# Issuing seven weight loads from GpSimd's queue instead of SyncE's, in a convolution and attention step

## The chip, the cores and the metric

The program runs on one core of a Trainium2 chip. The metric is the device time of one execution in microseconds (us), the median of several runs. Five engines run their own instruction streams in the order in which the program was scheduled: TensorE (PE, with PEld for its weight loads), VectorE (DVE), ScalarE (ACT), GpSimd (POOL) and SyncE (SP, which here does nothing but issue transfers). An engine that waits for an instruction's inputs lets nothing behind it in its stream pass. Transfers between the chip's memory and the on-chip buffer are issued from one of these streams and carried out by 16 DMA engines.

## The reference, cut to what matters

The program is one inference step of a two-layer decoder. The first layer is a gated convolution; the part that matters here is its end:

```python
h = _rmsnorm(x, g_norm)
val, glu_gate, z = jnp.split(h @ w_in, 3, axis=-1)
v = val * jax.nn.sigmoid(glu_gate)
c = depthwise_conv(v, 31 taps) + conv_b
c = jax.nn.silu(_layernorm(c, ln_g, ln_b))
y = (c * jax.nn.silu(z)) @ w_out        # (2080 x 2048) @ (2048 x 1024)
x1 = x + y
```

After it come a shared key/value product, dilated window attention in three groups and an output product, which the change does not touch. All values are float32.

## The kernel before, in words

**Precision.** A float32 product is made of three products in a format that TensorE reads at full rate. Each operand is split into a high part (a cast) and a low part (the rest). The output weights `w_out` arrive raw, tile by tile; ACT casts the high part (`ho`, line 262), and DVE or POOL subtracts to get the low part (`lo`, line 265). DVE takes both halves of the first tile and the second halves of the next three, POOL the others.

**Stages around the change.** Phase A computes the products of `w_in` and the convolution. Its last part, `tail`, multiplies the three last column tiles of z with the five chunks of x (`zchunk`, lines 73 to 77); ACT applies silu and issues the store. Between the chunks `phase_b` puts the first two row tiles through the layer norm. Phase B has 17 row tiles of 128 rows (the last but one has 32), in "positions" 0 to 16. For each position:

- `norm` loads c (`bc`, line 297) and silu(z) (`bsz`, line 303), reduces over channels (DVE, line 306), finishes the mean by a product with a matrix of constants (PE, line 308, into `bst`), subtracts (DVE, line 309), squares in two halves (ACT, line 312, into the one buffer `bsq`), reduces each half (DVE, line 314, `bv`), finishes the variance on PE (line 315), takes the root and reciprocal (ACT line 317, DVE line 318), multiplies (DVE, line 319), applies silu with gain and bias (ACT, line 321, 16 pieces) and multiplies with silu(z) (DVE, line 322).
- `split` makes the high part `bmh` (ACT, line 336) and the low part `bml` (DVE, line 337).
- `out` makes two output products of 48 matmuls each (lines 359 to 361, into `bpo`), one per half j of the 1024 output columns.

**The weights.** `w_out` is 2048 x 1024, cut into j = 0, 1 and four tiles each (h = 0 to 3), a tile being 1 MB. `Weights.ahead` (line 234) loads seven of these eight raw tiles in two transfers of 512 KB each; the eighth goes through a stage of its own in `Weights.half` (line 257). In the names below, the raw tiles of j = 0 are `rawo_9236`, `rawo_9239`, `rawo_9242` and `rawo_9245` with the high parts `ho_9248`, `ho_9254`, `ho_9260`, `ho_9266`; those of j = 1 are `rawo_9312`, `rawo_9315`, `rawo_9318`. `bc_8798`, `bc_8926`, `bc_9272`, `bc_9464` and `bc_9616` are the c tiles of positions 0, 1, 2, 3 and 4. The raw tiles lie in memory that x held in phase A. So the first can be loaded when chunk 0 of z is done, the other three of j = 0 when chunk 1 is done, and those of j = 1 when all of z is done.

**What sets the order.** A scheduler at build time plays the program through with a cost model and writes each engine's stream as it goes; nothing is reordered on the chip. Priorities steer it: loads and casts of weights are made with `high_priority(offset=1000)`. The variable `pace` holds the last transfer of a chain, and `issue_after(pace)` keeps a transfer behind that one. In the kernel before, the raw loads and the loads of c (line 297) are in this chain, all in SP's stream.

Of the kernel before, what the change touches and what calls it, by code (L numbers as in the profile page):

```python
# [224 lines left out]
class Weights:  # L225
# [8 lines left out]
    def ahead(self, src, nm, tag, pool=None):  # L234

        raw = (pool or self.pool).tile([128, 4, 512], F32, tag=tag, name=f"raw{nm}")
        with self.tc.high_priority(offset=1000):
            for q in range(2):
                with self.tc.issue_after(self.d["pace"].ins):
                    self.d["pace"] = self.nc.sync.dma_start(raw[:, 2 * q:2 * q + 2], src[q])  # L240
        return raw

    def half(self, src, nm, gain=None, pool=None, raws=None):
# [33 lines left out]
def phase_b(tc, d, kc, tail, outer, then):  # L277
# [6 lines left out]
    with ExitStack() as ctx:  # L284
# [90 lines left out]
        def ahead(c):  # L375
            if c < 2:
                cc[c] = norm(c)
                if c == 0:
                    ms[0] = split(0, cc[0])

        tail(ahead)
        pw = outer.enter_context(tc.tile_pool(name="w", bufs=1, side="right", reuse_waits="tile"))
        wts = Weights(tc, d, pw, outer.enter_context(tc.tile_pool(name="w_s", bufs=2, side="right", reuse_waits="tile")))
# [733 lines left out]
```

## Time and profile before

| | us |
|---|---|
| median of 3 runs | 3110.9 |
| lowest and highest | 3108.03, 3112.82 |
| the profiled execution | 3108.9 |
| its span in the trace | 3107.1 |
| PE busy in it | 2990.2 (96%) |
| DVE, ACT, POOL busy | 2187.3, 1517.9, 1281.0 |

The span is the time from the first to the last recorded instruction; the execution is 1.8 us longer. The page cuts the span into 40 slices of 77.7 us and shows PE's busy share of each in tenths. Five slices are below nine tenths: the first, while the input is prepared; the one from 1087.5 to 1165.2 us (seven tenths), in which phase A hands over to phase B; the one from 1320.6 us (seven tenths) in phase B; and two in the attention stage, the very last among them. The raw tiles are loaded in the hand-over, and the rows below are mostly of it and of the 100 us behind it.

### The profile page before, as it was taken

The page shows a single profiled execution, that of the slowest core. Times are in us where ns is not written, and L with a number is a line of the kernel's source. Part 1 is how long each engine was busy: PE and PEld are TensorE (multiplying, and loading weights), DVE is VectorE, ACT ScalarE, POOL GpSimd, SP SyncE. Part 2 cuts the span into 40 slices and gives each one's busy share as a digit, 9 for nine tenths or more (in the row PEclk, how much of TensorE's full clock was granted, in tenths as well). Part 3 has the DMA queues.
Part 4 walks back from the last instruction along what each step waited for, and adds up shares of the span by engine and source line. Part 5 has one row for each costly group of instructions (what it writes and reads, how often), then busy time and mean ns, then how long its engine had stood idle before and what let it go on. Part 6 is the DMA issues. An engine that isn't in the chain of part 4 may idle for free.

```text
span 3107.1 us, 43111 instructions
## 1 busy us (share of the span) xinstructions
PE 2990.2 (96%) x15994; PEld 2537.2 (82%) x15994; DVE 2187.3 (70%) x3698; ACT 1517.9 (49%) x2913; POOL 1281.0 (41%) x809
## 2 busy tenths in 40 slices
PE   6999999999999979999979999999999998999998
PEld 6999999999999977878756777767777776667786
DVE  6599999999999957667556565666666756445355
ACT  6544555554544355566544444554444633444432
POOL 1799889888877603000013222223332032002242
PEclk9999999999999999999999999999999999999999
DMA  7333334434331266444386666788766566653674
GB/s 196 99 107 100 121 106 144 139 112 134 112 128 64 79 194 192 125 133 119 99 211 183 168 164 171 174 232 212 180 162 153 171 189 187 186 182 116 247 258 161
DMA packets 563404, 482.41 MB, mean 155 GB/s; under 512 B 338321, under 2 KB 474129, under 8 KB 555641
## 3 DMA queue, kind: packets, MB, share of 16 engines
q1 hardware_dynamic: 560601, 475.64, 52.2%
q10 hardware_dynamic: 2592, 4.01, 0.4%
q8 instruction: 126, 2.06, 0.3%
q14 instruction: 85, 0.70, 0.1%
HBM read 345.42 MB, written 221.84 MB: 183 GB/s over the span
## 4 chain that ended last, share of the span: by engine, by line
PE 57%; DVE 14%; DMA 11%; POOL 9%; issue 4%; ACT 4%; SPq 1%; POOLq 0%; DVEq 0%; ACTq 0%
DVE acc L196 7%; POOL ca L181 7%; PE s L808 3%; PE pjk L536 3%; DMA qb<-t_qs 3%; PE pjk L539 2%; PE pjk L538 2%; PE pjv L536 2%; PE pt L827 2%; PE pjv L539 2%; PE ut L836 2%; PE pjv L538 2%; PE pjq L538 2%; PE pjq L536 2%; PE pjq L539 2%
## 5 line engine op out<-in xcount | busy, mean ns | idle before, releaser
L181 POOL TENSOR_TENSOR ca<-ca,tp 128x1024 f32<-128x1024 f32 x288 | 706.7, 2456 | 174.3 <-ACT tp L180 123.7
L196 DVE SCALAR_TENSOR_TENSOR acc<-vb,cws,acc 128x1024 f32<-128x1024 f32 x608 | 754.6, 1281 | 6.5
L180 ACT ACTIVATE tp<-vb,cws 128x1024 f32<-128x1024 f32 x288 | 329.7, 1151 | 286.3 <-POOL ca L181 277.5
L750 POOL COPY ro<-xt 128x512 f32<-128x512 f32 x128 | 151.8, 1193 | 381.8 <-DMA t_xt<-ro 168.6
L629 POOL TENSOR_TENSOR qb<-qb,kc 128x512 f32<-128x512 f32 x96 | 124.5, 1301 | 331.1 <-DMA qb<-t_qs 255.0
L68 PE MATMUL pg<-xh,wh 128*128 128x416 f32 x640 | 227.3, 355 | 2.0 <-ACT xh L151 1.9
L68 PE MATMUL pv<-xh,wh 128*128 128x416 f32 x640 | 225.6, 352 | 1.3 <-DVE vb L109 0.8
L69 PE MATMUL pg<-xl,wh 128*128 128x416 f32 x640 | 225.9, 353 | 0.1
L70 PE MATMUL pg<-xh,wl 128*128 128x416 f32 x640 | 225.9, 353 | 0.0
L68 PE MATMUL pz<-xh,wh 128*128 128x416 f32 x640 | 225.1, 352 | 0.0
L70 PE MATMUL pz<-xh,wl 128*128 128x416 f32 x640 | 224.7, 351 | 0.0
L70 PE MATMUL pv<-xh,wl 128*128 128x416 f32 x640 | 224.6, 351 | 0.0
L69 PE MATMUL pv<-xl,wh 128*128 128x416 f32 x640 | 224.3, 351 | 0.0
L69 PE MATMUL pz<-xl,wh 128*128 128x416 f32 x640 | 224.1, 350 | 0.0
L688 POOL MEMSET spq<- 128x24 f32 x8 | 0.9, 118 | 534.3 <-DMA t_x<-bx 371.9
L819 ACT ACTIVATE sm<-sm,ngm 128x256 f32<-128x256 f32 (+1 forms) x384 | 172.7, 452 | 92.5 <-DVE ngm L816 88.0
L359 PE MATMUL bpo<-ho,bmh 128*128 128x512 f32 x512 | 205.2, 403 | 11.4 <-ACT ho L262 7.8
L360 PE MATMUL bpo<-lo,bmh 128*128 128x512 f32 x512 | 204.2, 399 | 4.2 <-DVE lo L265 3.0
L361 PE MATMUL bpo<-ho,bml 128*128 128x512 f32 x512 | 202.5, 397 | 3.4 <-DVE bml L337 3.4
L830 ACT COPY qp_p<-pt 128x512 f32<-128x512 f32 x150 | 86.3, 584 | 179.9 <-PE pt L827 179.3
L536 PE MATMUL pjk<-hk,xt 128*128 128x512 f32 x384 | 161.5, 421 | 10.1 <-ACT xt L500 9.8
L536 PE MATMUL pjq<-hq,xt 128*128 128x512 f32 x384 | 155.4, 405 | 4.3 <-ACT hnk L547 4.3
(319 smaller groups left out, 7569.7 us busy)
## 6 DMA issues: line engine op xcount, KB each, us to landing
t_xt<-ro SPq DMA_DIRECT2D x128, 256.0 KB
xt<-t_xt SPq DMA_DIRECT2D x32, 1024.0 KB
wr<-in_win SPq DMA_DIRECT2D x48, 512.0 KB
qb<-t_qs SPq DMA_DIRECT2D x96, 256.0 KB
kc<-in_cache SPq DMA_DIRECT2D x72, 256.0 KB
vc<-in_cache SPq DMA_DIRECT2D x72, 256.0 KB
t_c<-ca SPq DMA_DIRECT2D x16, 1040.0 KB
bc<-t_c SPq DMA_DIRECT2D x16, 1024.0 KB
```

Of the source, the lines that this page charges most:

```text
L68: nc.tensor.matmul(ps, lhsT=hi[:, k], rhs=xh[:, k], start=(k == 0), stop=False)
L69: nc.tensor.matmul(ps, lhsT=hi[:, k], rhs=xl[:, k], start=False, stop=False)
L70: nc.tensor.matmul(ps, lhsT=lo[:, k], rhs=xh[:, k], start=False, stop=(k == 7))
L180: nc.scalar.activation(tp, src, AF.Copy, scale=cws[:, ct, j:j + 1])
L181: nc.gpsimd.tensor_tensor(dst, dst, tp, op=ALU.add)
L196: nc.vector.scalar_tensor_tensor(out if j == KT - 1 else acc[h], vt[:, h * 1024 + j:h * 1024 + j + 1024], cws[:, ct, j:j + 1], out if j == ...
L359: nc.tensor.matmul(po[:n], lhsT=mh[:, a], rhs=hi, start=(a == 0), stop=False)
L360: nc.tensor.matmul(po[:n], lhsT=mh[:, a], rhs=lo, start=False, stop=False)
L361: nc.tensor.matmul(po[:n], lhsT=ml[:, a], rhs=hi, start=False, stop=(a == 15))
L536: first = nc.tensor.matmul(ps[:n], lhsT=xh[:, j], rhs=hi[:, j], start=(k == 0), stop=False)
L538: nc.tensor.matmul(ps[:n], lhsT=xh[:, j], rhs=lo[:, j], start=False, stop=False)
L539: nc.tensor.matmul(ps[:n], lhsT=xl[:, j], rhs=hi[:, j], start=False, stop=(k == last))
```

## The change

The two transfers of each raw tile in `ahead` are issued from GpSimd's stream, and they leave the `pace` chain. They neither wait for the last transfer in the chain, nor does the next one wait for them.

```diff
@@ -236,8 +236,7 @@
         raw = (pool or self.pool).tile([128, 4, 512], F32, tag=tag, name=f"raw{nm}")
         with self.tc.high_priority(offset=1000):
             for q in range(2):
-                with self.tc.issue_after(self.d["pace"].ins):
-                    self.d["pace"] = self.nc.sync.dma_start(raw[:, 2 * q:2 * q + 2], src[q])
+                self.nc.gpsimd.dma_start(raw[:, 2 * q:2 * q + 2], src[q])
         return raw
```

The changed file is one line shorter, so its line numbers behind 239 are lower by one: line 308 of before is line 307 of after.

The scheduler now writes other streams on all engines. In GpSimd's stream the 14 transfers stand right behind the last low part of phase A's weights and ahead of every `lo` of the output weights. In SP's stream the load of `bc_9272` (position 2) follows directly on that of `bc_9464` (position 3); before, eight raw loads and a load of silu(z) stood between them.

PE, from the end of the z products, before:

```order
L359 MATMUL bpo_0_9360<-ho_9248,bmh_8838 128x512
L360 MATMUL bpo_0_9360<-lo_9249,bmh_8838 128x512
L361 MATMUL bpo_0_9360<-ho_9248,bml_8839 128x512
L359 MATMUL bpo_0_9360<-ho_9248,bmh_8838 128x512
L360 MATMUL bpo_0_9360<-lo_9249,bmh_8838 128x512
L361 MATMUL bpo_0_9360<-ho_9248,bml_8839 128x512
L359 MATMUL bpo_0_9360<-ho_9248,bmh_8838 128x512
L360 MATMUL bpo_0_9360<-lo_9249,bmh_8838 128x512
```

The same place on PE after the change (`bst_9278` and `bst_9471` belong to the norms of positions 2 and 3):

```order
L358 MATMUL bpo_0_9360<-ho_9248,bmh_8838 128x512
L359 MATMUL bpo_0_9360<-lo_9249,bmh_8838 128x512
L360 MATMUL bpo_0_9360<-ho_9248,bml_8839 128x512
L307 MATMUL bst_9278<-bs_9276,ones 128x128
L307 MATMUL bst_9471<-bs_9469,ones 128x128
L358 MATMUL bpo_0_9360<-ho_9248,bmh_8838 128x512
L314 MATMUL bst_9278<-bv_0_9283,ones 128x128
L359 MATMUL bpo_0_9360<-lo_9249,bmh_8838 128x512
```

The first of these rows is the fourth matmul of the product; three like it stand ahead of it. The last three of the four `L314` rows (the second of `bst_9278`, both of `bst_9471`) stand behind the 18th matmul (two) and the 19th (one), and `bst_9622<-bs_9620` (position 4) behind the 48th, ahead of the second product. Before, all 48 matmuls came first, and then the two rows of `L308` for positions 2 and 3.

DVE, from the low part of the first output tile, before:

```order
L265 TENSOR_TENSOR lo_9249<-rawo_9236,ho_9248 128x1024 x2
L337 TENSOR_TENSOR bml_9350<-bc_8926,bmh_9349 128x2048
L265 TENSOR_TENSOR lo_9255<-rawo_9239,ho_9254 128x1024
L265 TENSOR_TENSOR lo_9261<-rawo_9242,ho_9260 128x1024
L265 TENSOR_TENSOR lo_9267<-rawo_9245,ho_9266 128x1024
L306 TENSOR_REDUCE bs_9276<-bc_9272 128x128
L309 TENSOR_TENSOR bc_9272<-bc_9272,bst_9278 128x2048
```

The same place on DVE after the change:

```order
L264 TENSOR_TENSOR lo_9249<-rawo_9236,ho_9248 128x1024
L336 TENSOR_TENSOR bml_9350<-bc_8926,bmh_9349 128x2048
L305 TENSOR_REDUCE bs_9276<-bc_9272 128x128
L264 TENSOR_TENSOR lo_9261<-rawo_9242,ho_9260 128x1024
L308 TENSOR_TENSOR bc_9272<-bc_9272,bst_9278 128x2048
L308 TENSOR_TENSOR bc_9464<-bc_9464,bst_9471 128x2048
L313 TENSOR_REDUCE bv_0_9283<-bsq_0_9281 128x128
L264 TENSOR_TENSOR lo_9249<-rawo_9236,ho_9248 128x1024
L313 TENSOR_REDUCE bv_1_9288<-bsq_1_9286 128x128
L313 TENSOR_REDUCE bv_0_9476<-bsq_0_9474 128x128
L313 TENSOR_REDUCE bv_1_9481<-bsq_1_9479 128x128
L264 TENSOR_TENSOR lo_9255<-rawo_9239,ho_9254 128x1024
```

The second half of `lo_9249`, which the 8th matmul needs, now stands behind the first three steps of two norms. Next come the two reciprocals, the multiplication of position 2, the second half of `lo_9267`, the multiplication of position 3 and the reduction `bs_9620` of position 4.

ACT, from the first cast of an output tile, before:

```order
L262 CAST ho_9248<-rawo_9236 128x1024 x2
L336 CAST bmh_9349<-bc_8926 128x2048
L262 CAST ho_9254<-rawo_9239 128x1024 x2
L262 CAST ho_9260<-rawo_9242 128x1024 x2
L262 CAST ho_9266<-rawo_9245 128x1024 x2
```

The same place on ACT after the change:

```order
L261 CAST ho_9248<-rawo_9236 128x1024
L335 CAST bmh_9349<-bc_8926 128x2048
L261 CAST ho_9254<-rawo_9239 128x1024
L261 CAST ho_9266<-rawo_9245 128x1024
L261 CAST ho_9260<-rawo_9242 128x1024 x2
L311 ACTIVATE bsq_0_9281<-bc_9272 128x1024
L261 CAST ho_9248<-rawo_9236 128x1024
L311 ACTIVATE bsq_1_9286<-bc_9272 128x1024
L311 ACTIVATE bsq_0_9474<-bc_9464 128x1024
L311 ACTIVATE bsq_1_9479<-bc_9464 128x1024
L261 CAST ho_9254<-rawo_9239 128x1024
```

The second half of `ho_9248` moved behind the first square of position 2, and that of `ho_9254` behind all four squares of positions 2 and 3.

## Rows read from the trace of the kernel before

**Rows 1.** Windows: us; busy of PE, PEld, DVE, ACT, POOL; PE clock; DMA; GB/s.
```profile
1146.00:1176.00 30.00, 15.35 (x51) 11.01 (x52) 24.02 (x9) 18.44 (x28) 12.43 (x4) 0.76 1.10 353
1176.00:1203.00 27.00, 27.00 (x119) 22.22 (x118) 22.16 (x14) 17.79 (x29) 16.96 (x8) 0.95 0.52 173
1203.00:1240.00 37.00, 32.96 (x133) 25.61 (x132) 25.40 (x15) 20.68 (x41) 0.00 (x0) 0.91 0.60 171
1240.00:1560.00 320.00, 312.80 (x1397) 252.93 (x1395) 206.65 (x154) 188.09 (x351) 0.00 (x0) 1.00 0.42 119
```
**Rows 2.** PE's timeline: start, us, instruction, [idle before <-releaser].
```profile
1153.72 0.79 PE L359 MATMUL bpo<-ho,bmh 128*128 128x512 f32 x1 [7.85 <-ACT ho L262]
1157.47 0.79 PE L360 MATMUL bpo<-lo,bmh 128*128 128x512 f32 x1 [2.96 <-DVE lo L265]
...
1159.34 0.63 PE L361 MATMUL bpo<-ho,bml 128*128 128x512 f32 x1
...
1175.29 1.13 PE L308 MATMUL bst<-bs,ones 128*128 128x128 f32 x4 [2.77 <-DVE bs L306]
1176.08 1.20 PE L359 MATMUL bpo<-ho,bmh 128*128 128x512 f32 x2
...
1568.78 0.79 PE L536 MATMUL pjk<-hk,xt 128*128 128x512 f32 x1 [9.16 <-ACT xt L500]
```
**Rows 3.** The timeline of SP's stream of transfers, 1101 to 1164 us.
```profile
1101.12 36.62 SPq L303 DMA_DIRECT2D bsz<-t_sz  x2
...
1143.95 0.36 SPq L297 DMA_DIRECT2D bc<-t_c  x1
1144.43 13.63 SPq L240 DMA_DIRECT2D rawo<-in_wout  x8
...
1161.93 1.88 SPq L297 DMA_DIRECT2D bc<-t_c  x1
```
**Rows 4.** ACT's timeline, four rows from 1099 to 1186 us.
```profile
1099.04 0.52 ACT L76 ACTIVATE st<-pz 128x416 f32<-128x416 f32 x1 [4.02 <-PE pz L70]
...
1152.62 1.99 ACT L262 CAST ho<-rawo 128x1024 fp32r<-128x1024 f32 x2 [0.50 <-ACT st L76]
...
1172.78 1.05 ACT L262 CAST ho<-rawo 128x1024 fp32r<-128x1024 f32 x1 [8.82 <-DMA rawo<-in_wout]
...
1184.47 1.03 ACT L312 ACTIVATE bsq<-bc 128x1024 f32<-128x1024 f32 x1 [1.29 <-DVE bv L314]
```
**Rows 5.** DVE's timeline, eight rows from 1108 to 1192 us.
```profile
1108.75 3.75 DVE L306 TENSOR_REDUCE bs<-bc 128x128 f32<-128x2048 f32 x1 [3.88 <-DMA bc<-t_c]
...
1156.20 2.35 DVE L265 TENSOR_TENSOR lo<-rawo,ho 128x1024 fp32r<-128x1024 f32 x2
1158.47 2.28 DVE L337 TENSOR_TENSOR bml<-bc,bmh 128x2048 fp32r<-128x2048 f32 x1
1160.67 10.08 DVE L265 TENSOR_TENSOR lo<-rawo,ho 128x1024 fp32r<-128x1024 f32 x3
1171.43 3.71 DVE L306 TENSOR_REDUCE bs<-bc 128x128 f32<-128x2048 f32 x1 [0.68 <-DMA bc<-t_c]
1176.04 4.49 DVE L309 TENSOR_TENSOR bc<-bc,bst 128x2048 f32<-128x2048 f32 x2 [0.89 <-PE bst L308]
1180.44 1.22 DVE L314 TENSOR_REDUCE bv<-bsq 128x128 f32<-128x1024 f32 x1
...
1190.39 0.95 DVE L318 RECIPROCAL br<-br 128x128 f32<-128x128 f32 x1 [1.30 <-ACT br L317]
```
**Rows 6.** DMA queues in the window 1172 to 1180 us: packets, MB, share.
```profile
q1 hardware_dynamic: 902, 3.28, 102.6%
```
**Rows 7.** DMA queues in the window 1102.3 to 1104.4 us, SP's (q1), ACT's (q10).
```profile
q1 hardware_dynamic: 1001, 0.50, 84.9%
q10 hardware_dynamic: 142, 0.21, 29.0%
```
**Rows 8.** POOL's timeline, the first low parts of the output weights.
```profile
1159.29 10.39 POOL L265 TENSOR_TENSOR lo<-rawo,ho 128x1024 fp32r<-128x1024 f32 x3 [84.12 <-ACT ho L262]
```

## The prediction

> **What bounds the kernel now.** I read the windows by stage first, then PE's waits in the poorest of them, then what the engines named there were doing, and last the streams of transfers. The windows [rows 1] show where there is anything to gain or lose. In the 30 us after the z products PE is busy for 15.35 us at a granted clock of 0.76; in the next 27 us it is never idle; in the 37 us behind them it lacks 4.0 us (37.00 - 32.96), at a clock of 0.91; in the 320 us after 1240 it lacks 7.2 us. So the hand-over costs about 15 us of idle PE, and what follows is bound by PE.
>
> PE's timeline [rows 2] says what the idle time was. The first wait, 7.85 us up to 1153.72, ends with ACT's cast `ho`. It does not end with a load: ACT's row for that cast [rows 4] starts at 1152.62 behind ACT's own `st`, in the order of its stream. The second, 2.96 us, ends with DVE's `lo`, itself behind a reduction and a multiplication. Only then comes the third, 2.77 us before the `bst` product at 1175.29.
>
> Transfers are late in two places only. DVE's reduction of position 2 (`bc_9272`) starts at 1171.43, when its load lands [rows 5], and ACT is idle for 8.82 us until the raw tiles of j = 1 are there at 1172.78 [rows 4]. SP's stream [rows 3] tells why: it stood at a load of silu(z) for 36.62 us until 1137.7, issued the c tile of position 3 at 1143.95, then eight raw transfers in 13.63 us, and reached `bc_9272` only at 1161.93.
>
> **The change, part by part.** *Issue.* 14 issues leave SP. The ones that could run early do: chunk 1 of z is done at about 1099.04 [rows 4], so seven transfers of 0.524 MB (3.67 MB) start then, some 45 us earlier than at 1144.43. This gains nothing at the first product's start, since ACT's order sets that. On POOL the issues fall into an idle stretch of 84.12 us [rows 8]. No row shows what one costs there: between 0 and the 1.70 us of SP's (13.63 / 8), 14 of them take 0 to 24 us of POOL, most of it ahead of 1159. POOL's `lo` of `ho_9254` stands behind all 14, the last of which wait for the end of z (1145.9 by PE's row at 1153.72 less 7.85): six issues from there last until 1146 to 1156. I take no cost.
>
> *Loads beside each other.* The c tile of position 1 lands at 1108.75, and DVE had waited 3.88 us for it [rows 5]; PE's `bst` of it stands inside the z products. Now 3.67 MB go beside it. At the 410 GB/s of raw loads (3.28 MB in 8 us, [rows 6]) that is 8.9 us of the DMA engines: the upper end, if the c tile waits for all of it. The lower end is 0. The nearest row is of two queues beside each other [rows 7]: the second queue took 0.21 of 0.71 MB, 30%. Of the 9.7 us from 1099.04 to 1108.75 that is 2.9 us: **+3 us** at the end of z.
>
> The Trainium skill bears on this (*DMA: Bandwidth & Descriptors*, section *SWDGE vs HWDGE vs iDMA*): inside each DMA engine the hardware and GpSimd's software queues are served round-robin. The row differs from one packet each in turn: 142 packets passed beside 1001. By the skill's rule with larger packets on GpSimd's side the c tile would wait nearly the whole 8.9 us.
>
> *The order.* This is the large term. SP now issues `bc_9272` right behind `bc_9464`, so the scheduler finds the c tiles of positions 2 and 3 early and writes their norms into the first output product. PE's stream has two `bst` behind the 6th matmul, `bst` again behind the 7th, two behind the 18th, one behind the 19th. These are engines in order, so each such row is a wait of PE for DVE and ACT. In before's clock, from rows 5 unless noted:
>
> 1. PE's sixth matmul ends at 1159.97 [rows 2]. DVE's `bml` ends at 1158.47 + 2.28 = 1160.75. `bc_9272` has landed: two c tiles of 1.05 MB at the 341 GB/s of rows 7 (0.71 MB in 2.1 us) take 6.2 us from 1143.95, and six raw transfers beside them (3.15 MB at 410) another 7.7, to 1157.9.
> 2. DVE's reduction: 3.71, to 1164.5. PE's two `bst`: to 1165.0, after 4.5 us of waiting.
> 3. DVE's `lo_9261` at 3.36 (10.08 / 3, POOL working beside it): 1167.8. Subtraction 2.25 (4.49 / 2): 1170.1. ACT's square 1.03 and cast 1.05 [rows 4]: 1172.2. Only now has the 7th matmul its `ho_9248`: PE waited 7.2 us.
> 4. DVE: the other subtraction to 1172.3, a variance reduction 1.22 to 1173.5, the second half of `lo_9249` (2.35 / 2) to 1174.7, three more variance reductions. The squares share one buffer, so a pair costs 1.03 + 1.22 = 2.25: about 1175.8, 1178.1, 1180.4. PE has its last `bst` at 1180.6.
> 5. ACT casts the second half of `ho_9254` behind the last square; DVE makes `lo_9255` by 1181.7. That is the 20th of 48 matmuls; 29 are left.
> 6. DVE: two reciprocals of 0.95, to 1183.6; a multiplication of some 2.3 (as `bml`, of the same shape) and up to 1 more for POOL beside it, to 1186.5; `lo_9267`, to 1187.7. PE has its next 24 at 0.23 (27.00 / 119, [rows 1]) by 1187.2, and the last five by 1188.8.
> 7. DVE: the multiplication of position 3 to 1190.0, the reduction of position 4 to 1193.7; PE's `bst` for it stands ahead of the second product, which starts at 1194.3.
>
> Before, it started at 1176.08 [rows 2]. **Lag: 18.2 us**, with the loads 21.2. The skeptical end: if the casts hidden by these waits are ready early and the clock no worse, half of steps 3 to 6 is still forced by data, about 9. The other end: with 42 matmuls at half clock, 0.23 us more for each, 9.7 us more, 28.
>
> *What is given back.* The norms of positions 2 and 3 are done some 10 us earlier, relative to the products, than before. So the idle 4.0 us of 1203 to 1240 go [rows 1], as they wait for such norms. The clock of 0.91 there is 18% of 37 us at half speed (6.7 us), which costs 3.3 us; that goes with the idleness. Of the 7.2 us after 1240 I take 2, with bounds 0 and 7.2. Together -9.3 (bounds -4 and -14.5). The eighth raw tile and the j = 1 casts are cast later on ACT, 0 to 4 us; I take 0, since the second product covers them. At the start of the attention stage PE waits 9.16 us for ACT, up to 1568.78 [rows 2]. If what it waits for were independent of the products, up to 9.16 us of lag would vanish there; it is the transposed x1, which the last products make, so I take 0.
>
> Sum: 3 + 18.2 - 9.3 = **+11.9** on the profiled execution's 3108.9: 3120.8. That execution is 2.0 us under the median of the runs (3110.9), so the forecast is **3123 us**.
>
> The skill also has a rule under which nothing of this follows: DMAs from any engine run on the same 16 DMA engines, and issuing from several saves only the sequencer's time (*DMA: Bandwidth & Descriptors*, section *Issuing engines are not separate DMA queues*). The trace differs in one respect: the raw transfers sat behind a wait of 36.62 us in SP's stream, which is order and not issue time [rows 3].
>
> **The rivals.**
>
> *No change to speak of (3108 to 3117).* The norms have to be done anyway, and DVE and ACT have slack later: DVE is busy 206.65 of the 320 us after 1240 [rows 1]. If all the 14.5 us come back and half or none of the lag is covered, the sum is 3 + 9 to 18 - 14.5, -2 to +7; what is above that can still vanish in the 9.16 us at 1568.78. For it: the same work is only moved. Against it: PE lacks only 7.2 us after 1240, so a lag that is left at 1240 has little to be taken out of. If the order mattered little and only issue time were saved, the effect would be the same, as SP's issues are not on PE's path.
>
> *Faster (3104 or below).* The place is positions 2 to 5: norms early enough that no `bst`, `bmh` or `bml` is waited for until the attention stage, 4.0 + 7.2 + 3.3 = 14.5 us gained, with the 2.77 of 1175.29 gone as well, 17.3. It decides when the stalls in the first product are below that less 6.2, about 11; with stalls of 8 the time is 3110.9 + 8 - 17.3 = 3102. For it: both rows that were late on a transfer (1171.43, 1172.78) get theirs 10 us earlier. Against it: steps 2 to 5 are data dependences in PE's stream, 12 us by step 3 alone.
>
> *Much slower (3132).* The raw loads crowd out the c tile of position 1 (8.9 instead of 3) and, with PE idle in pieces, the clock stays at half for the first product (+9.7 at most, 3 taken): 3123 + 5.9 + 3 = 3132. For it: the clock was 0.76 in 1146 to 1176 with PE half idle. Against it: rows 7, where the second queue took 30%.
>
> **How the numbers follow.** Forecast 0.50; much slower 0.20; no change 0.18; faster 0.12. A measurement can tell about 0.2%, 6.2 us, from no change, so "same" is 3104.7 to 3117.1. Faster then 0.11, same 0.19 (with the edge of the faster case), slower 0.70. The range takes the forecast's own spread (3111 to 3135: 3123 less half of the 18.2 us and 3 for the loads, and 9.7 and 2.3 more at half clock) and reaches down into "no change" and up past the crowding: 3107 to 3138. The slow cases' own range is 3115 to 3138.
>
> **What would show it.** Right: PE's rows after the sixth matmul wait 4 to 8 us each for DVE's `bs` and ACT's `ho`; the first product takes about 35 us instead of 22; the second starts 15 to 25 us later; windows behind it have less idle time and a full clock. The raw loads run at 1099 to 1109, and DVE's reduction of position 1 starts at 1110 to 1114. Wrong: `bst` without a wait in the first product; a second product that starts by 1185; or the lag coming back in the attention stage.

## The result, and the profile after

The changed kernel takes 3141.56 us (median of 4 runs, 3138.08 to 3147.2) against 3110.46 in the same session: a ratio of 1.0095 with an interval of 1.0084 to 1.0107, 31.1 us slower. The forecast was 3123 with a range of 3107 to 3138. The direction was right, the size was not. The profiled execution is the slowest of the four, 3147.2 us with a span of 3145.4.

Comparing two traces needs one correction. Starts in phase A, which the change does not touch, differ between executions: ACT's `st` at 1072.6 us in the trace of before stands 6.1 us later in that of after, and between 1.6 us earlier and 7.2 us later in the kernels below. On PE and ACT the order of instructions up to there is the same in all these kernels. A shift in this document is a start in one trace less that in the trace of before, less this offset.

Three windows of after that answer to [rows 1], and two that follow the same work (columns as there):

```profile
1146.00:1176.00 30.00, 19.91 (x94) 17.90 (x93) 17.55 (x9) 22.81 (x41) 2.11 (x4) 0.83 0.74 237
1176.00:1203.00 27.00, 11.30 (x37) 8.35 (x38) 24.52 (x13) 11.25 (x13) 7.99 (x5) 0.62 0.61 165
1203.00:1240.00 37.00, 32.72 (x133) 26.43 (x131) 21.07 (x12) 23.74 (x47) 23.56 (x8) 0.91 0.32 86
...
1235.00:1272.00 37.00, 37.00 (x166) 30.48 (x165) 21.63 (x14) 17.73 (x31) 0.00 (x0) 1.00 0.47 139
1269.50:1589.50 320.00, 312.60 (x1390) 252.27 (x1388) 204.45 (x153) 183.52 (x338) 0.00 (x0) 0.99 0.42 119
```

The 27 us in which PE was never idle before are now its poorest: 11.30 busy at a clock of 0.62. The window at 1235 answers to [rows 1]'s window at 1203: its 4 idle us are gone, as forecast, and PE does 166 matmuls in it instead of 133. The 320 us behind it (1269.5, before 1240) lack 7.4 us, before 7.2: nothing was gained there.

PE's timeline after, the waits of the first output product and ahead of the second (answers to [rows 2]):

```profile
1168.30 0.79 PE L358 MATMUL bpo<-ho,bmh 128*128 128x512 f32 x1 [5.68 <-ACT ho L261]
1172.33 0.80 PE L359 MATMUL bpo<-lo,bmh 128*128 128x512 f32 x1 [3.24 <-DVE lo L264]
1179.13 1.19 PE L307 MATMUL bst<-bs,ones 128*128 128x128 f32 x4 [4.30 <-DVE bs L305]
1190.74 0.80 PE L358 MATMUL bpo<-ho,bmh 128*128 128x512 f32 x1 [10.42 <-ACT ho L261]
...
1211.34 0.77 PE L307 MATMUL bst<-bs,ones 128*128 128x128 f32 x2 [4.28 <-DVE bs L305]
```

The two large waits are the ones that the order made: `bst` of positions 2 and 3 at 1179.13, and the seventh matmul at 1190.74, whose cast stands on ACT behind a square. ACT's row for that square says whom it waits for:

```profile
1188.70 1.03 ACT L311 ACTIVATE bsq<-bc 128x1024 f32<-128x1024 f32 x1 [11.78 <-DVE bc L308]
1189.66 1.03 ACT L261 CAST ho<-rawo 128x1024 fp32r<-128x1024 f32 x1
```

DVE's timeline after (answers to [rows 5]):

```profile
1106.32 3.67 DVE L305 TENSOR_REDUCE bs<-bc 128x128 f32<-128x2048 f32 x1 [14.91 <-DMA bc<-t_c]
1123.51 3.58 DVE L305 TENSOR_REDUCE bs<-bc 128x128 f32<-128x2048 f32 x1 [13.52 <-DMA bc<-t_c]
...
1175.37 3.62 DVE L305 TENSOR_REDUCE bs<-bc 128x128 f32<-128x2048 f32 x1
1178.90 7.57 DVE L264 TENSOR_TENSOR lo<-rawo,ho 128x1024 fp32r<-128x1024 f32 x1
```

The second row is position 1: it starts at 1123.51 (before 1108.75), and DVE waited 13.52 us for the c tile instead of 3.88. POOL's timeline after, the issues and the first low parts (answers to [rows 8]):

```profile
1091.67 0.72 POOL L239 DMA_DIRECT2D rawo<-in_wout  x1 [10.36 <-PE pz L70]
1105.45 3.66 POOL L239 DMA_DIRECT2D rawo<-in_wout  x7 [13.06 <-PE pz L70]
1162.83 2.25 POOL L239 DMA_DIRECT2D rawo<-in_wout  x4 [53.72 <-PE pz L70]
1177.34 1.08 POOL L239 DMA_DIRECT2D rawo<-in_wout  x2 [12.26 <-DMA rawo<-in_wout]
1178.44 6.94 POOL L264 TENSOR_TENSOR lo<-rawo,ho 128x1024 fp32r<-128x1024 f32 x3
```

One load starts when chunk 0 is done, seven more at 1105.45, as soon as chunk 1 is done. An issue costs POOL 0.52 us (3.66 / 7). The first low part stands behind all 14, of which the last two waited for a transfer until 1177.34. It starts 0.46 us ahead of DVE's `lo` at 1178.90, and that one lasts until 1.09 us after POOL's three are done (1186.47 and 1185.38). SP's stream (answers to [rows 3]) and the DMA queues from 1105 to 1124 us, with two rows of issues (the columns there: KB of one, median us to landing):

```profile
1105.94 46.40 SPq L302 DMA_DIRECT2D bsz<-t_sz  x2
1158.61 2.39 SPq L296 DMA_DIRECT2D bc<-t_c  x2
1161.10 4.37 SPq L256 DMA_DIRECT2D rawo<-in_wout  x2
```
```profile
q1 hardware_dynamic: 5112, 2.60, 52.2%
q0 software_dynamic: 1008, 3.67, 49.0%
...
rawo<-in_wout POOLq DMA_DIRECT2D x7, 512.0 KB, 10.0
...
t_sz<-st ACTq DMA_DIRECT2D x2, 208.0 KB
```

GpSimd's queue (q0) moves 3.67 MB in 1008 packets of 3.6 KB; SP's packets, with the c tile, are of 0.5 KB. The raw loads are in after 10.0 us, while the c tile takes until 1123.5.

In the attention stage, PE's waits of after from 1594 to 2060 us (engine, line, waited for, us in total, times, longest):

```profile
PE pjq L535 <- ACT hnk L546: 8.4, 1, 8.4
```

Where the time is lost, by shifts: end of z +8.5, taken at ACT's last `st` (PE's own last z matmul is 10.6 late, but PE's wait behind it is 2.2 us shorter, 5.68 instead of 7.85); the first output product +21.1 more (the second starts at 1211.76, not 1176.08 as in [rows 2]: 35.7, less 6.1 and 8.5); 7.6 back by the start of the ninth output product on PE and 1.3 of that lost again by the last, which leaves 23.3; attention, from the first to the last `xt` of its first group (1568 to 1996 us), +4.6; the rest, +4.2, lies behind that. These are 32.1 us between two executions, behind phase A; the medians are 31.1 apart.

### The profile page after: what moved, and what is told of

Its sections match the earlier page's. It is cut to its first block, busy times and chain, and to the rows that moved or that the text cites. A ratio compares the mean times of both kernels' runs of the same rounds, so it can differ in the third digit from the quotient of the medians.

```text
span 3145.4 us, 43122 instructions
## 1 busy us (share of the span) xinstructions
PE 3000.9 (95%) x15994; PEld 2543.1 (81%) x15994; DVE 2178.5 (69%) x3698; ACT 1519.4 (48%) x2913; POOL 1288.2 (41%) x823
## 4 chain that ended last, share of the span: by engine, by line
PE 72%; DMA 10%; DVE 9%; ACT 3%; POOL 3%; issue 2%; SPq 0%; POOLq 0%; ACTq 0%; DVEq 0%
PE pz L70 3%; PE pz L68 3%; PE pz L69 3%; PE pg L68 3%; PE s L807 3%; PE pg L70 3%; PE pg L69 3%; PE pv L68 3%; PE pv L70 3%; PE pv L69 3%; PE pjk L535 3%; DMA qb<-t_qs 3%; PE pjk L538 2%; PE pjk L537 2%; PE pjv L535 2%; PE pjq L535 2%
```

## The experiments

The account under test ("theory A") has three places of loss: the raw loads beside the c tile of position 1, the norms inside the first output product, and the order at the start of the attention stage. The expectations give rivals letters of their own and say what each is. The table has all runs: median and ratio against before in the same session, and shifts (start of DVE's reduction of position 1; end of z, by ACT's last `st`; end of the output products, by DVE's last addition to one; the change from there to the last `xt` of attention's first group). Each shift is of the one profiled execution of its kernel.

| run | median | ratio [interval] | reduction 1 | z | outputs | attention |
|---|---|---|---|---|---|---|
| after | 3141.6 | 1.0095 [1.0084, 1.0107] | 8.7 | 8.5 | 23.3 | +4.6 |
| e1_order | 3125.2 | 1.0044 [1.0022, 1.0066] | 9.1 | 8.8 | 8.8 | +0.1 |
| e2_late | 3123.4 | 1.0047 [1.0031, 1.0063] | -1.1 | -1.2 | 1.3 | +6.1 |
| e3_both | 3122.5 | 1.0038 [1.002, 1.0055] | -1.2 | -1.4 | 8.4 | -0.6 |
| e4_dummy | 3120.8 | 1.0036 [1.0025, 1.0048] | 8.1 | 7.9 | 7.9 | +1.0 |
| e5_attn | 3142.0 | 1.009 [1.0069, 1.011] | 10.0 | 9.7 | 18.2 | +7.0 |
| e6_dose | 3114.5 | 1.0005 [0.9993, 1.0017] | 3.0 | 2.7 | 2.9 | +1.7 |
| e7_j1 | 3125.0 | 1.004 [1.0026, 1.0054] | -1.4 | -1.6 | 6.4 | +7.3 |
| e8_late_attn | 3120.8 | 1.0026 [1.0016, 1.0036] | -1.9 | -1.9 | 3.6 | +4.3 |
| e9_paced | 3127.6 | 1.0047 [1.0029, 1.0066] | 10.1 | 9.8 | 9.9 | +3.6 |
| e10_paced_late | 3136.7 | 1.0075 [1.0057, 1.0094] | 0.8 | 0.8 | 18.9 | +5.7 |
| e11_sp | 3126.0 | 1.0045 [1.0028, 1.0062] | 1.6 | 1.5 | 13.2 | +5.3 |
| e12_dummy_act | 3115.7 | 1.0008 [0.9999, 1.0018] | 6.4 | 6.1 | 4.4 | +0.3 |
| e13_late_attn2 | 3125.1 | 1.0045 [1.0029, 1.0061] | -1.6 | -1.8 | 0.9 | +2.3 |

Before was 3109.7 for e1 to e4, 3112.2 for e5 to e8, 3112.0 for e9 to e12 and 3110.6 for e13. Single runs of one kernel lie up to 17.5 us apart (e7), so a median of a few says little under 5 us; the shifts decide.

**1. The loads alone.** The kernel before, with seven extra raw loads from GpSimd into free memory; then with three.

```diff
+            if pos == 0:
+                extra = [pm.tile([128, 4, 512], F32, tag=tag, name=f"ex{tag}") for tag in ("mh0", "ml0")]
+                for t in extra:
+                    nc.gpsimd.tensor_copy(t[:1, :, :1], c[:1, :4, :1])
+                for k in range(7):      # e6_dose: range(3)
+                    nc.gpsimd.dma_start(extra[k // 2 % 2][:, k % 2 * 2:k % 2 * 2 + 2], wout[k // 4, k % 4][0])
```

> The kernel before the change, with seven more loads of 512 KB from GpSimd's queue into memory that is free then, issued when the c tile of position 0 has landed; nothing reads them. The order of TensorE's stream is that of before. It measures the cost of the loads beside the c tile of position 1 alone. Theory A: the c tile of position 1 lands 6 to 13 us later, TensorE waits for its sum, the time is 3115 to 3124 us. Rival B (such loads cost nothing, only the order does): 3108 to 3113 us.

> The kernel before the change with three extra loads of 512 KB from GpSimd's queue beside the c tile of position 1, instead of the seven of the run named e4_dummy. Theory A (what counts is the bytes that go ahead of the c tile, 1.3 us for each load at 410 GB/s): the c tile lands about 3.5 to 4.5 us late instead of 8.1, the time is 3112 to 3116 us. Rival F (a fixed cost as soon as GpSimd's queue is in use): 7 to 9 us late as with seven, 3117 to 3122 us.

DVE's row for position 1 with seven loads:

```profile
1120.85 3.58 DVE L312 TENSOR_REDUCE bs<-bc 128x128 f32<-128x2048 f32 x1 [14.61 <-DMA bc<-t_c]
```

PE's order is that of before, and yet the reduction comes 8.1 us later and stays so to the end of the outputs (7.9): nothing behind it makes up for it. Three loads, 1.57 MB, cost 3.0, half a microsecond less than expected, and a time that cannot be told from before's. By these shifts the loss goes by bytes, 1.9 to 2.2 us for each MB, and a fixed cost (rival F) is out.

**2. The same from ScalarE.** Is it GpSimd's software queue?

```diff
-                    nc.gpsimd.dma_start(extra[...], ...)   # and the copies
+                    nc.scalar.dma_start(extra[...], ...)
```

> The kernel before with seven extra raw loads into free memory, issued by ScalarE's hardware queue (they were issued by GpSimd's in an earlier run, where position 1's reduction came 8 us later). They start when the c tile of position 0 has landed, beside that of position 1. Theory A1 (any large loads beside it crowd the c tile, by bytes): the reduction of position 1 comes 6 to 9 us later, 3115 to 3124. Theory A2 (only GpSimd's software queue pushes the c tile aside; a second hardware queue takes 30% as in the profile of before): 1 to 4 us later, 3110 to 3116.

ACT's and DVE's timelines:

```profile
1101.02 0.86 ACTq L303 DMA_DIRECT2D exmh<-in_wout  x2
1101.97 1.28 ACTq L303 DMA_DIRECT2D exml<-in_wout  x2
...
1119.38 0.82 ACTq L303 DMA_DIRECT2D exmh<-in_wout  x2
```
```profile
1113.51 3.58 DVE L312 TENSOR_REDUCE bs<-bc 128x128 f32<-128x2048 f32 x1 [9.15 <-DMA bc<-t_c]
```

Only four loads, 2.10 MB, ran ahead of the reduction, and it came 6.4 us later by the shift. The first c tile was itself 1.1 us late in this execution; from SP's issue of the tile of position 1 to its reduction it is 16.70 us against 12.45 before (1096.30 to 1108.75), 4.3 more. The same measure gives 4.6 for the three loads of e6 and 9.6 for the seven of e4. So for each MB ScalarE's loads cost 3.0 us by the shift and 2.0 by this measure, GpSimd's 1.9 to 2.2 and 2.6 to 2.9: a hardware queue delays the tile as well, but which of the two costs more for each byte stays open, and with four loads for seven the two expectations are not cleanly parted. The time is not told apart from before's.

**3. The loads held back.** The loads of the first four tiles wait on GpSimd, by a copy of four numbers for each tile, for the reduction of position 1; they are also queued in the order of the tiles.

```diff
-                self.nc.gpsimd.dma_start(raw[:, 2 * q:2 * q + 2], src[q])
+                with ExitStack() as behind:
+                    if "pool" in self.d:
+                        behind.enter_context(self.tc.issue_after(self.d["pool"].ins))
+                    if q == 0 and nm in ("o00", "o01", "o02", "o03"):
+                        self.nc.gpsimd.tensor_copy(raw[:1, :, :1], self.d["sums"][1][:1, :4].unsqueeze(2))
+                    self.d["pool"] = self.nc.gpsimd.dma_start(raw[:, 2 * q:2 * q + 2], src[q])
```

> The changed kernel with the raw loads of j = 0 held on GpSimd's queue until the channel sum of position 1 exists (a four-element copy from it into the raw tile), so that none runs beside the c tile of position 1; the raw loads are queued in tile order. The scheduler still puts the norms of positions 2 and 3 into the first output product, behind the 24th matmul instead of the 6th. Theory A: the z products end within 3 us of the kernel before, the norms still cost 5 to 15 us, the time is 3115 to 3128 us. Rival B (only the order costs): 3130 to 3142 us. Rival C (only the loads cost): 3106 to 3113 us.

DVE's row for position 1:

```profile
1111.66 3.69 DVE L310 TENSOR_REDUCE bs<-bc 128x128 f32<-128x2048 f32 x1 [4.79 <-DMA bc<-t_c]
```

The wait is 4.79 us as before's 3.88, the loss at the end of z is gone (-1.2), and the outputs lose only 1.3, though the norms still stand in the first product, behind its 24th matmul: the second product starts 11.9 us later than z alone explains, and 9.3 of that is back by the sixth. What is left is in attention (+6.1). The expected time was met by luck: the norms cost less by the end of the outputs than the 5 to 15 us expected, and attention was not in that sum.

**4. The norms moved out of the first product.** Two edges put the first `bst` of positions 2 and 3 behind the 48th matmul, where they stand before the change.

```diff
-            nc.tensor.matmul(ps[:, 0, :n], lhsT=kc.ones, rhs=s, start=True, stop=True)
+            means[pos] = nc.tensor.matmul(ps[:, 0, :n], lhsT=kc.ones, rhs=s, start=True, stop=True)
+            # and, for positions 2 and 3, an edge behind the last matmul of the first product
```

> The changed kernel with two issue-order edges on TensorE: the mean products of positions 2 and 3 stand behind the 48th matmul of the first output product, as before the change. The seven early raw loads from GpSimd's queue stay. Theory A (two costs that add: about 12 us from the loads beside the c tile of position 1, about 12 us net from the norms inside the first product, the rest behind it): the z products still end 10 to 15 us late, the first product loses its inner waits, the time is 3118 to 3128 us. Rival B (only the order costs; the late z end is the order's too): 3106 to 3115 us. Rival C (only the loads cost, all that is lost in the first product comes back anyway): 3138 to 3144 us.

The outputs end 8.8 us late, just what the end of z already had: the 14.8 us are gone. PE's longest wait is now

```profile
1184.98 0.80 PE L361 MATMUL bpo<-lo,bmh 128*128 128x512 f32 x1 [9.36 <-DVE lo L264]
```

and is made up later. (e1's z was expected 10 to 15 us late.) Both edits together:

> Both edits of the two runs before in one kernel: raw loads from GpSimd's queue, held until the channel sum of position 1, and the norms behind the first product. Theory A: both costs gone, 3104 to 3114 us, the time of before within a few us. Rival D (loads from GpSimd's queue cost by themselves, by their descriptors or by the engine's time): above 3120 us.

That missed. The end of z is at -1.4, but PE's timeline has two other waits:

```profile
1170.31 0.80 PE L367 MATMUL bpo<-lo,bmh 128*128 128x512 f32 x1 [9.48 <-DVE lo L269]
...
1221.79 0.80 PE L366 MATMUL bpo<-ho,bmh 128*128 128x512 f32 x1 [4.38 <-ACT bmh L343]
```

The outputs end at 8.4. That is within 0.4 us of e1, whose z ended 10.2 us later: in these two kernels, which differ only in how the loads are held, when z ends hardly matters. So e1 shows what the order does to PE's waits, and e4, not e1, that a late z stays. That the late norms are then the bound is argued from these waits, not tested. The two losses do not simply add, since each hides some of the other. By its time e3 lies in rival D's range, as does e7 below. But nothing is late at the end of its z, and e11 below loses as much without a load on GpSimd, so rival D is not needed; none of these runs excludes a smaller part of it.

**5. The change in halves.** Only the tiles of j = 1 on GpSimd (the others as before); all tiles out of the chain but on SP; all on GpSimd but still in the scheduler's chain; and the last with the loads held back as in 3.

```diff
 e7:   if nm.startswith("o1"): self.nc.gpsimd.dma_start(...)   # else as before
 e11:  self.nc.sync.dma_start(raw[:, 2 * q:2 * q + 2], src[q])  # no issue_after
 e9:   with self.tc.issue_after(self.d["pace"].ins):
           self.d["pace"] = self.nc.gpsimd.dma_start(raw[:, 2 * q:2 * q + 2], src[q])
```

> One part of the change alone: only the three raw tiles of j = 1 come from GpSimd's queue; those of j = 0 stay in SyncE's stream. They can't run before the z products end, and the norms of positions 2 and 3 stand behind the first output product. Theory A: no late c tile of position 1, no waits of the mean products inside the first product, but hk stands ahead of hnk in the attention stage (4 to 8 us): 3110 to 3120 us. Rival D (loads from GpSimd's queue cost by themselves): above 3122 us.

> The loads are issued from GpSimd's queue, but they stay in the chain that the scheduler plans with, so that the order of the engines is almost that of before (the two mean products of positions 2 and 3 stand behind the 36th matmul of the first output product instead of the 48th); on the chip GpSimd still issues the first seven as soon as their memory is free. Theory A (three costs: loads beside the c tile, norms inside the first product, order of the attention stage): about 8 us at the reduction of position 1 stay, the waits inside the first product shrink to 0 to 4 us, and the attention stage loses 4 to 7 us if its order is that of after (GpSimd's queue in it is the same as after's here): 3118 to 3130. Rival B (issuing from GpSimd is itself what costs, whatever the order): 3138 or more. Rival C (only the order costs, the loads beside the c tile are made up later): 3108 to 3116.

> As the kernel with the chain kept, and the first four raw tiles are held on GpSimd behind a copy of four numbers that needs the reduction of position 1, so that no raw load runs beside the c tile of position 1. Theory A: nothing at the end of z (within 2 us of before), 0 to 5 us in the first products, 4 to 7 us in the attention stage: 3112 to 3123. Rival C (loads beside the c tile cost nothing in the end): the same time as the kernel with the chain kept, within 3 us.

> The loads leave the chain but stay in SyncE's queue: the other half of the change alone. SyncE's stream still stands at the load of silu(z) until z's second last chunk, so no raw load runs beside the c tile of position 1, and the c tile of position 2 is behind all the raw loads. Theory A: nothing at the end of z (within 2 us), no mean product inside the first output product, 4 to 8 us at most in the attention stage, whose order is that of after: 3111 to 3121. Rival B' (leaving the chain is what costs, whatever the queue): 3130 or more.

PE's waits up to 1250 us in e7, then in e9, e10 and e11 up to 1300:

```profile
PE bst L318 <- DVE bv L317: 12.5, 1, 12.5
```
```profile
PE bpo L359 <- ACT ho L262: 8.0, 3, 5.1
PE bpo L360 <- DVE lo L265: 7.6, 3, 3.1
```
```profile
PE bst L311 <- DVE bs L308: 12.9, 1, 12.9
PE bpo L363 <- DVE lo L267: 10.9, 3, 6.6
```
```profile
PE bpo L359 <- DVE lo L264: 11.0, 2, 5.5
PE bpo L358 <- ACT ho L261: 7.2, 1, 7.2
```

e9 came near theory A by the end of the outputs: 9.8 us at the end of z (about 8 expected), nothing more in the outputs, 3.6 in attention (4 to 7). In between, its second product starts 7.5 us later than its first and makes that up. The other three missed. None of them delays the c tile of position 1, and still the outputs lose 6 to 19 us, each by another wait: a `bst` behind a variance (e7), behind a mean (e10), low parts (e11). In e11 SP's stream suggests a cause, which no run isolates: the c tile of position 2 stands behind all the raw loads.

```profile
1144.70 17.27 SPq L239 DMA_DIRECT2D rawo<-in_wout  x14
1162.08 0.39 SPq L296 DMA_DIRECT2D bc<-t_c  x1
```

So neither leaving the queue nor leaving the chain is *the* cost. Each edit makes the scheduler write another order at the hand-over, and from the end of z to that of the outputs these orders cost from nothing (e1, e4, e6, e9) over 2.5 to 5.5 (e2, e8, e13) to 18.1 (e10).

**6. The attention stage.** ACT's casts of the second key weight tile stand ahead of the first head norm in after; an edge puts them behind it. The same is then done on e2.

```diff
+                      with ExitStack() as behind:
+                        if nm.startswith("k1"):
+                            behind.enter_context(self.tc.issue_after(self.d["first"].ins))
```

> The changed kernel with one issue-order edge far behind the change, on ScalarE at the start of the attention stage: the casts of the second group's first key weights (hk) stand behind the first evacuation of a key product (hnk) instead of ahead of it. The two early costs stay. Theory A, third term (the changed order lets hk, which waits 3.6 us for its load, hold hnk and with it the first query product, so that TensorE waits 8.4 us there instead of 4.3 and then runs longer at half clock): the wait falls to about 4.5 us, the attention stage loses no more than 2 us against the kernel before up to its first score tiles, the time falls from 3141.6 to 3133 to 3138 us. Rival E (the attention stage's loss comes from other differences of the order, or from run to run): no change, 3138 to 3145 us.

> The kernel of e2_late (raw loads from GpSimd's queue, those of j = 0 held until the channel sum of position 1) with the edge of e5_attn on ScalarE. Theory A: the late c tile and the attention stage's loss are both gone, what is left is what the norms inside the first product cost at the end of phase B, 2 to 5 us: 3111 to 3118 us, against 3123.4 without the edge. Rival E: 3120 to 3126 us.

PE's waits in before from 1565 to 2025 us, then in e5 from 1590 to 1660:

```profile
PE pjq L536 <- ACT hnk L547: 4.3, 1, 4.3
```
```profile
PE pkt L781 <- DVE hnk L567: 5.2, 2, 4.5
PE pjq L538 <- ACT hnk L549: 3.9, 1, 3.9
```

The wait of `pjq` halves (8.4 to 3.9), and `pkt`, four transposes behind it, waits 4.5 instead: the loss stayed, and both e5 and e8 came out in the range of rival E.

The streams of e5 are those of after up to that place, so it is also a second look at the first output product. Its DVE and PE there:

```profile
1175.55 1.22 DVE L264 TENSOR_TENSOR lo<-rawo,ho 128x1024 fp32r<-128x1024 f32 x1
```
```profile
1181.04 0.80 PE L361 MATMUL bpo<-ho,bmh 128*128 128x512 f32 x1 [4.06 <-ACT ho L261]
```

DVE's `lo` is ahead of POOL's first (which starts at 1176.11) by 0.56 us, takes 1.22 us instead of 7.57, and PE's seventh matmul waits 4.06 instead of 10.42. The lag of the second product is then 16.0 and the outputs end at 18.2 instead of 23.3. So which of the two gets its turn first decides over 6.3 us here. It is not rare: in e1, where POOL's three start at 1175.76, DVE's next takes 7.91 us.

```profile
1175.88 7.91 DVE L264 TENSOR_TENSOR lo<-rawo,ho 128x1024 fp32r<-128x1024 f32 x1
```

In e9 one took 8.26 us although its start, 1172.65, is recorded 0.17 us ahead of POOL's three, so a lead that small does not tell which one waits. The profiled execution of after is its slowest of four; whether the others have this wait, no trace shows.

The last run restores the place of those transposes too: they go behind the ninth matmul of the sample rows' values, as before.

```diff
+                if nm == "vs0" and k == 4:
+                    # edge: the first key transposes behind this matmul
```

> As the kernel with the four late raw tiles and with the casts of the next weights behind the first head norm; one edge more puts the first four key transposes of the attention stage behind the ninth value product of the sample rows, where they stand in the kernel before (TensorE's order from there is then that of before for about 150 instructions). Theory A: the loss in the attention stage (6 us by the 16th key tile in the kernel without this edge) lies in these two places of the order together, so 0 to 3 us are left there, nothing at the end of z, 0 to 4 in the output products: 3111 to 3117. Rival E (the loss is not in this order; a wait moves to the next place, as it did before): 4 us or more in the attention stage again, 3118 to 3125.

PE's waits in e13 from 1574 to 2040 us:

```profile
PE pjq L546 <- ACT hnk L557: 4.0, 1, 4.0
...
PE pkt L789 <- DVE hnk L575: 1.1, 1, 1.1
```

Both waits are small now, and the loss in attention falls from 6.1 (e2) and 4.3 (e8) to 2.3, as theory A has it. The time did not follow: 3125.1, where 3111 to 3117 was expected. The outputs end 0.9 us late and the last `xt` 3.2, but the end of this trace is 11.6 late. Where that comes from is not settled: between the last `xt` and the end most kernels lose 1 to 8 us, with no edit there, and no run isolates it. Even e4 and e6, in which PE's order there is that of before, lose 2.6 and 5.6. The sorting by order is clear, though: the five kernels in which PE starts attention in before's order (e1, e3, e4, e6, e12) show -0.6 to 1.7, the eight in which it starts in after's 3.6 to 7.3.

No version beat the kernel before.

## Why the prediction was wrong, point by point

**What bounds the kernel, and the lag of the first output product: right.** PE's waits stand where the prediction put them, and e1 shows that the order makes them: none of its waits there is for a `bst`. The start of the second product was forecast 18.2 us later than the loads alone make it; it measured 21.1 in after and 16.0 in e5, with the same streams. The wait for the two `bst` (4.5) measured 4.30. That of the seventh matmul (7.2) measured 10.42 and 4.06: step 3 took `lo_9261` at 3.36 us, as in [rows 5], where DVE's three and POOL's three alternate, and neither execution has that. In one DVE comes first (1.22), in the other it waits for all three of POOL's (7.57).

The step on *issue* took no cost on POOL, with six issues done by 1156. The last two waited for a transfer until 1177.34, and POOL's first `lo` came 4.5 us later than before (1178.44 less 6.1 and 8.5, against 1159.29): in this trace that start falls just ahead of DVE's `lo`. The step also read 1.70 us for one issue of SP's out of a row that merges eight issues with the time between them. One by one they are short (ns: least, median, most):

```profile
L240 SPq DMA_DIRECT2D rawo<-in_wout x14: 322/420/2677, 1144.4 to 1168.5; - x14
```

The Trainium skill (*SBUF — State Buffer*, section *SBUF: two separate sides*) says that a VectorE operation with two inputs in this memory and a GpSimd operation that reads it exclude each other, the first one holding the ports for its whole instruction. The traces of after and e5 agree on who comes first, that of e9 (8.26 us) does not by its recorded starts; that POOL keeps its turn over three instructions is in the 7.57 us and not in the rule.

**Loads beside each other: the first step that failed.** "+3" was 8.5. The nearest row was misread: the second queue in [rows 7] moved 0.21 MB, but the store that it carried is 208 KB, as the issue row above says. That queue had no more to send; the row shows its whole transfer, not its share against a rival. With 3.67 MB waiting, the c tile lost 8.7 us, close to the prediction's upper end of 8.9, and e6 scales it with bytes. The Trainium skill's rule that the prediction set beside the row (*DMA: Bandwidth & Descriptors*, section *SWDGE vs HWDGE vs iDMA*) gave nearly 8.9, and the trace agrees; e12 shows that a second hardware queue delays the tile too. The rival "much slower" had this mechanism and priced it well (5.9 more), with a chance of 0.20. Its other part, a low clock in the first product, showed as well (0.62 from 1176 to 1203, before 0.95); what that cost is not told apart from the waits.

**What is given back: the second.** Of 9.3 us, 6.3 came by the end of the outputs. The first two terms were right: the 4.0 idle us of [rows 1] at 1203 and the 3.3 of their clock make 7.3, and 7.6 were back at the ninth output product (33 more matmuls in the window, at 0.23 us). What failed is the third term: where 2 us more were to come, 1.3 were lost. PE's waits of after from 1240 to 1590 us:

```profile
PE bst L314 <- DVE bv L313: 6.8, 4, 2.5
```

The step took 2 us out of the idle time of before behind 1240, as if the new order had none of its own there; it has as much (7.4 us for 7.2).

**The attention stage: the third.** It was forecast at 0 because what PE waits for is the transposed x1. That wait is unchanged (9.16 us in [rows 2], 9.1 after), but the prediction looked at no other order there. The streams differ some 450 us behind the edit: +4.6. That the order is the cause rests on the sorting above and, in part, on e13, which takes 3.8 of e2's 6.1 us away. The section on the profile had pointed elsewhere: the poor slice that it puts at 1320.6 us is the page's slice from 1553.5 to 1631.2 (62.01 of 77.7 us busy), the very start of attention.

The sum: 8.5 + 21.1 - 6.3 + 4.6 = 27.9, and 4.2 us behind that no run pins down, make the 32.1 between the two executions. Against the forecast's terms that is +5.5, +2.9, +3.0 and +4.6: no single step carries the miss, the loads weigh most, and all four went the same way. That after's profiled execution lost the race between DVE and POOL is in the +2.9; in e5, which did not, that term is -2.2.

**The rivals.** "No change" needed all of 14.5 us back; 6.3 came. "Faster" needed stalls below 11 us in the first product; the lag was 16 to 21.

## What to carry to other kernels

A transfer that is moved out of a queue in which it waited also starts earlier, beside whatever is on the path then; price it at all of its bytes before the transfer that matters (8.9 us here, 8.7 measured), unless a row shows two queues that both had work left. Hold such loads back with a small dependence on the critical tile (e2 took the 8.5 us back so), and look in the whole new order for what moved, not only near the edit. Before idle time is booked as a gain, check that the new order has no idle time of its own in its place.

## What the runs showed of the hardware that was not expected

- An issue of 512 KB costs GpSimd 0.52 us (3.66 / 7); SyncE's median for the same transfers is 0.42.
- Large transfers from ScalarE's queue delay the c tile as those from GpSimd's do: by the two measures 4.3 to 6.4 us for 2.10 MB, against 3.0 to 4.6 for 1.57 and 8.1 to 9.6 for 3.67.
- A VectorE subtraction of 1.22 us took 7.57 where three of GpSimd's had started 0.46 us ahead of it, and 8.26 in e9 where they are recorded 0.17 us behind it.
- Executions of the same kernel differ by some 10 us without any edit, and phase A alone by up to 8.8 us between kernels that do the same there.
